# A depthwise convolution whose running sums move to PSUM and whose diagonals move to GpSimd

## The chip, the core and the metric

The kernel runs on one core of one Trainium2 chip. The metric is the device time of one execution in microseconds: the median of three runs of the kernel before is 2928.71 us (2927.53 to 2931.35). The text uses the profile's names of the engines: PE is the matrix engine, PEld its weight load, DVE the vector engine, ACT the scalar engine, POOL is GpSimd, SP issues the loads of the weights.

## The reference

The program is a chain of three blocks over 256 tokens of width 1024, in float32. The change is in the convolution module of the second block:

```
a, gate = split(x @ w_in + b_in)          # 1024 -> 2 x 1024
h = a * sigmoid(gate)
h[t, ch] = b_dw[ch] + sum over w = 0..30 of w_dw[w, ch] * h[t - 30 + w, ch]   # depthwise
h = silu(layer_norm(h)) ;  out = h @ w_out + b_out
```

Everything ahead of it (a feed-forward layer) and behind it stays as it is.

## The kernel before

The module works with channels on partitions: 1024 channels are 8 blocks (`cb`) of 128, and the free dimension is time. `hp` holds for each block 30 zeros and then the 256 gated values, so a tap `w` of the convolution is the slice `hp[:, cb, w:w+256]`, times one weight per partition (`wd`). Four ways of summing the 31 taps are used beside each other:

- blocks 0 to 3, and 23 taps of block 4, on DVE: a chain of instructions, each of which multiplies a tap with its weight and adds the sum so far (`chain`, L1127 and L1131); the sum `y` lies in SBUF;
- block 5 on ACT and POOL: ACT multiplies a tap into a small buffer (three of them, L1163), POOL adds it to `y` (L1166);
- blocks 6 and 7, and 8 taps of block 4, on PE: 70 products with diagonal matrices `dg` that hold the weights, added up in PSUM (`pc`, L1171). DVE builds 30 of these diagonals (L1147), ACT 40 (L1153).

The input product comes in two ways. `stat_pairs` streams eight weight chunks. The first two (the lead) are multiplied for each half of the tokens as soon as its norm is done, and turned by PE transposes (L284); the other six are multiplied as pairs of 2 x 24 matmuls (`mm3`: each product as three, L117 to L119). Each chunk is loaded by SP into `raw` (three buffers), rounded by ACT to `wh` (L99) and the rest computed as `wl` (L101), in two halves: on DVE for chunks 0 to 2, on POOL for chunks 3 to 7. After each pair ACT takes the sigmoid (`sg`, L1150), DVE makes `hp` (L1151), and `advance(12)` traces 12 steps of the chains, in turn over all of them. The pair's PSUM buffer (`acc`, four of them) comes free only behind `hp`.

Behind the sums, 16 transposes (L1180) bring `y` back to tokens on partitions, the layer norm follows (ACT, DVE, and small POOL operations), then the output product, whose first two chunks have their `wl` on POOL.

Tiles are allocated by tag with a fixed number of buffers. A planner orders each engine's queue ahead of the run, by the order in which the code traces the instructions and by its own clock; `issue_after(x)` forbids that instructions traced in its block come ahead of `x` on `x`'s engine. On the chip each queue runs in order. Ahead of the module, `pre_norm` of the second token half ends with two small POOL operations (`rstd`, L147 and L150), on which its transposes wait.

Of the kernel before, what the change touches and what calls it, by code (L numbers as in the profile page):

```python
# [7 lines left out]
F32 = mybir.dt.float32  # L8
# [6 lines left out]
AF = mybir.ActivationFunctionType  # L15
OP = mybir.AluOpType
# [3 lines left out]
S = 256  # L20
D = 1024
# [1020 lines left out]
class Block2:  # L1042
# [61 lines left out]
    def conv(self):  # L1104
        k, nc, a = self.k, self.k.nc, self.k.a
        with ExitStack() as ctx:
            k.temp(ctx, "cvt")
            pool = ctx.enter_context(k.tc.tile_pool(name="cv", bufs=1))
            tl = lambda n, sh, dt=F32: pool.tile(sh, dt, name=n)
            par, wd = tl("par", [128, 3, 8]), tl("wd", [128, 8, 31])  # L1110
            nc.scalar.dma_start(par, a["conv_par"])
            nc.scalar.dma_start(wd, a["conv_dw"])
            lng, lnb, bout = (k.row(n) for n in ("conv_ln_g", "conv_ln_b", "conv_b_out"))
            hp = tl("hp", [128, 8, S + 30])
            nc.gpsimd.memset(hp[:, :, 0:30], 0.0)
            y = tl("y", [128, 8, S])
            xs = [tl(f"xs{t}", [128, D]) for t in range(2)]


            diag = {cb: tl(f"dg{cb}", [128, n, 128]) for cb, n in ((6, 31), (7, 31), (4, 8))}  # L1120
            fill = [(cb, w) for cb in diag for w in range(diag[cb].shape[1])]
            tap = lambda cb, w: hp[:, cb, w:w + S]
            chains = []

            def chain(cb):
                w0 = 8 if cb == 4 else 0
                nc.vector.tensor_scalar(y[:, cb], tap(cb, w0), wd[:, cb, w0:w0 + 1], par[:, 2, cb:cb + 1],  # L1127
                                        op0=OP.mult, op1=OP.add)
                yield
                for w in range(w0 + 1, 31):  # L1130
                    nc.vector.scalar_tensor_tensor(y[:, cb], tap(cb, w), wd[:, cb, w:w + 1], y[:, cb],  # L1131
                                                   op0=OP.mult, op1=OP.add)
                    yield

            def advance(n):

                while n > 0 and chains:
                    c = chains.pop(0)
                    if next(c, 1) is None:
                        chains.append(c)  # L1140
                        n -= 1

            pairs = k.stat_pairs(lambda cb: k.stream(a["conv_in"][cb], pool=cb > 2), 8,
                                 2, lambda c, t: xs[t][:, c * 256:c * 256 + 256])
            with k.tc.issue_after(k.done.ins):
                for b, w in fill[:30]:
                    nc.vector.tensor_scalar(diag[b][:, w], k.ident, wd[:, b, w:w + 1], None, op0=OP.mult)  # L1147
            for cb, (pa, pg) in enumerate(pairs):
                sg = k.tmp.tile([128, S], F32, tag="sg", name="sg")
                ins = nc.scalar.activation(sg, pg, AF.Sigmoid, bias=par[:, 1, cb:cb + 1])  # L1150
                nc.vector.scalar_tensor_tensor(hp[:, cb, 30:], pa, par[:, 0, cb:cb + 1], sg, op0=OP.add, op1=OP.mult)  # L1151
                for b, w in fill[30 + cb * 5:35 + cb * 5]:
                    nc.scalar.activation(diag[b][:, w], k.ident, AF.Copy, scale=wd[:, b, w:w + 1])  # L1153
                if cb < 5:
                    chains.append(chain(cb))
                advance(12)
            scratch = k.sm.tile([128, 1], F32, tag="va", name="scratch")
            nc.scalar.activation(scratch, hp[:, 7, 30:31], AF.Silu)
            with k.tc.issue_after(ins.ins):
                cb = 5  # L1160
                for w in range(31):
                    p = k.tmp.tile([128, S], F32, tag="tap", name="tap", bufs=3) if w else y[:, cb]
                    nc.scalar.activation(p, tap(cb, w), AF.Identity, scale=wd[:, cb, w:w + 1],  # L1163
                                         bias=0.0 if w else par[:, 2, cb:cb + 1])
                    if w:
                        nc.gpsimd.tensor_tensor(y[:, cb], y[:, cb], p, op=OP.add)  # L1166
            for cb in diag:
                n = diag[cb].shape[1]
                pc = k.acc((128, S), "pc")
                for w in range(n):  # L1170
                    nc.tensor.matmul(pc, diag[cb][:, w], tap(cb, w), start=w == 0, stop=w == n - 1)  # L1171
                if cb != 4:
                    nc.scalar.activation(y[:, cb], pc, AF.Identity, bias=par[:, 2, cb:cb + 1])
            advance(155)
            nc.vector.tensor_tensor(y[:, 4], y[:, 4], pc, op=OP.add)
            pts, nms = [], []
            for t in range(2):
                pts.append([k.tp(name="pt") for h in range(2)])
                for cb in range(8):
                    nc.tensor.transpose(pts[t][cb // 4][:, cb % 4], y[:, cb, t * 128:t * 128 + 128], k.ident)  # L1180
                nm = k.sm.tile([128, 1], F32, tag="nm", name="nm")
                sums = k.sm.tile([128, 2], F32, tag="sums", name="sums")
                x = [p.rearrange("p i c -> p (i c)") for p in pts[t]]
                nc.scalar.activation(xs[t][:, 0:512], x[0], AF.Identity, accum_out=sums[:, 0:1])
                nc.vector.tensor_reduce(sums[:, 1:2], x[1], axis=AX.X, op=OP.add)
                nc.vector.tensor_scalar(nm, sums[:, 0:1], sums[:, 1:2], -1.0 / D, op0=OP.add, op1=OP.mult)
                nms.append(nm)
            for t in range(2):
                nm = nms[t]
                ss = k.sm.tile([128, 2], F32, tag="ss", name="ss")  # L1190
                z, sq = k.xn(), k.xn()
                x, u, g, b = ([p.rearrange("p i c -> p (i c)") for p in pts[t]], k.halves(z), k.halves(lng), k.halves(lnb))
                for h, q in enumerate(k.halves(sq)):
                    nc.scalar.activation(q, x[h], AF.Square, bias=nm, accum_out=ss[:, h:h + 1])
                    nc.vector.scalar_tensor_tensor(u[h], x[h], nm, g[h], op0=OP.add, op1=OP.mult)
                sv = k.sm.tile([128, 1], F32, tag="nv", name="nv")
                nc.gpsimd.tensor_tensor(sv, ss[:, 0:1], ss[:, 1:2], op=OP.add)
                r = k.rsqrt_n(sv, D, 1)
                for h, o in enumerate(k.halves(xs[t])):
                    nc.vector.scalar_tensor_tensor(u[h], u[h], r, b[h], op0=OP.mult, op1=OP.add)  # L1200
                    nc.scalar.activation(o, u[h], AF.Silu)
                    k.to_T(o, k.xh, k.xl, t, 4, kb0=h * 4)
                if t == 0:
                    after = k.done
            g3, gn = self.gain(0, 3), self.gain(0, 4)

            def done(t, acc):
                u = [xs[t][:, h * 512:(h + 1) * 512] for h in range(2)]
                for h in range(2):
                    nc.vector.tensor_tensor(u[h], acc[h], bout[:, h * 512:(h + 1) * 512], op=OP.add)  # L1210
                k.post_norm(t, u, g3, 1.0, gn)
            k.last = after
            k.linear_rows(a["conv_out"], k.xh, k.xl, done, tail=2, pool=2)
            k.last = None
# [146 lines left out]
class Block3:  # L1361
# [257 lines left out]
    def mix(self, l, nt):  # L1619
        k, nc, a = self.k, self.k.nc, self.k.a  # L1620
        with ExitStack() as ctx:
# [15 lines left out]
            def attention():  # L1637
                flush()
                for t in (2, 0, 1)[3 - nt:]:
                    yield from self.attention(l, t, sink, ga)  # L1640
            side, conv = attention(), self.conv(l, nt)
            weave(iter(lambda: next(conv, True), True), side, lambda i: 2)
            for _ in side:
                pass
# [225 lines left out]
```

## Time and profile before

| | |
|---|---|
| median of three runs | 2928.71 us |
| the profiled execution's own time | 2930.06 us |
| its span | 2928.3 us |
| PE busy in the span | 2782.8 us (95%) |
| DVE | 1808.6 us (62%) |
| ACT | 1362.3 us (47%) |
| POOL | 437.6 us (15%) |
| granted clock of PE, mean | 0.972 |

Busy time is of one profiled execution. Matmuls overlap, so a busy PE counts each one's whole duration; the distance of two starts is what one costs in a dense row. A number in brackets behind a row is how long the engine sat idle before it and what ended that. "L1131" is a line of the kernel before.

### The profile page before, as it was taken

To read this page: it belongs to the slowest core of one execution; us is meant where nothing else is said; L and a number is where in the kernel's file an instruction comes from. 1 tells how busy PE (TensorE), PEld (TensorE's weight loads), DVE (VectorE), ACT (ScalarE), POOL (GpSimd) and SP (SyncE) were. 2 spreads that over 40 slices of the span, in tenths; PEclk is the share of its full clock that TensorE was granted. 3 is DMA by queue.
4 is the path that set the end of the run, shared out by engine and by line. 5 is a ranking of instruction groups with operands and counts; after the bars stand their busy time and mean duration, and the time that the engine had idled before them with its cause. 6 is when DMAs were issued, how large, how long until landed. Compare 5 with 4: busy or idle time off the path is not lost.

```text
span 2928.3 us, 44693 instructions
## 1 busy us (share of the span) xinstructions
PE 2782.8 (95%) x18182; PEld 2498.8 (85%) x18182; DVE 1808.6 (62%) x2984; ACT 1362.3 (47%) x2318; POOL 437.6 (15%) x338
## 2 busy tenths in 40 slices
PE   8999978899999999998599999999999999999999
PEld 6787978899999888987489899897998878888897
DVE  6646789785555556549765465676655564464654
ACT  4544535544444555435344454524445344453543
POOL 2101766500000000006600000051001010000100
PEclk9999989999999999999799999999999999998999
DMA  5424436696666555554055465524554334442453
GB/s 201 170 72 146 152 129 226 234 336 227 213 206 206 196 188 212 187 187 145 8 197 184 166 214 185 194 89 151 195 187 164 104 107 158 157 143 101 153 189 106
DMA packets 105982, 496.74 MB, mean 170 GB/s; under 512 B 11040, under 2 KB 44320, under 8 KB 50224
## 3 DMA queue, kind: packets, MB, share of 16 engines
q1 hardware_dynamic: 61632, 443.15, 43.7%
q10 hardware_dynamic: 44144, 50.74, 5.2%
q8 instruction: 142, 2.33, 0.3%
q14 instruction: 64, 0.52, 0.0%
HBM read 476.03 MB, written 17.83 MB: 169 GB/s over the span
## 4 chain that ended last, share of the span: by engine, by line
PE 58%; issue 23%; DVE 10%; POOL 4%; DMA 2%; ACT 2%; POOLq 0%; ACTq 0%; DVEq 0%; SPq 0%
PE acc L117 6%; PE acc L119 6%; PE acc L118 6%; PE o L987 4%; PE o L986 4%; PE o L989 4%; PE tp L117 3%; PE tp L119 3%; PE tp L118 3%; PE o L316 2%; DVE y L1131 2%; PE o L319 2%; PE o L317 2%; PE tp L409 2%; DVE A L950 1%
## 5 line engine op out<-in xcount | busy, mean ns | idle before, releaser
L101 DVE TENSOR_TENSOR wl<-raw,wh 128x1024 fp32r<-128x1024 f32 x764 | 914.8, 1218 | 618.3 <-ACT wh L99 617.4
L99 ACT CAST wh<-raw 128x1024 fp32r<-128x1024 f32 x848 | 861.6, 1041 | 709.7 <-PE acc L118 219.1
L117 PE MATMUL acc<-xx,wh 128*128 128x256 f32 x1504 | 423.9, 282 | 3.7 <-DVE hp L1151 3.7
L119 PE MATMUL acc<-xx,wl 128*128 128x256 f32 x1504 | 423.9, 282 | 2.2 <-POOL wl L101 1.4
L118 PE MATMUL acc<-xx,wh 128*128 128x256 f32 x1504 | 424.3, 282 | 0.0
L117 PE MATMUL tp<-xx,wh 128*128 128x256 f32 (+1 forms) x1440 | 413.3, 287 | 5.3 <-ACT ga L970 5.3
L119 PE MATMUL tp<-xx,wl 128*128 128x256 f32 (+1 forms) x1440 | 411.1, 285 | 0.8 <-POOL wl L101 0.8
L118 PE MATMUL tp<-xx,wh 128*128 128x256 f32 (+1 forms) x1440 | 410.9, 285 | 0.0
L147 POOL TENSOR_SCALAR va<-ss 128x1 f32<-128x1 f32 (+1 forms) x49 | 24.6, 502 | 1815.6 <-ACT junk L143 1632.4
L117 PEld LDWEIGHTS acc<-xx,wh 128*128 128x128 f32 x1504 | 285.5, 190 | 3.9 <-issue 3.9
L119 PEld LDWEIGHTS acc<-xx,wl 128*128 128x128 f32 x1504 | 285.6, 190 | 2.6 <-POOL wl L101 1.6
L117 PEld LDWEIGHTS tp<-xx,wh 128*128 128x128 f32 x1440 | 276.6, 192 | 8.8 <-ACT ga L970 5.7
L118 PEld LDWEIGHTS acc<-xx,wh 128*128 128x128 f32 x1504 | 283.8, 189 | 0.0
L118 PEld LDWEIGHTS tp<-xx,wh 128*128 128x128 f32 x1440 | 276.9, 192 | 2.4
L119 PEld LDWEIGHTS tp<-xx,wl 128*128 128x128 f32 x1440 | 276.3, 192 | 1.1 <-POOL wl L101 1.0
L101 POOL TENSOR_TENSOR wl<-raw,wh 128x1024 fp32r<-128x1024 f32 x84 | 236.2, 2836 | 127.1 <-ACT wh L99 127.1
L117 PE MATMUL acc<-wh,xx 128*128 128x256 f32 (+2 forms) x672 | 226.3, 338 | 3.2 <-ACT xx L112 3.2
L118 PE MATMUL acc<-wl,xx 128*128 128x256 f32 (+2 forms) x672 | 221.6, 331 | 4.1 <-DVE wl L101 4.1
L119 PE MATMUL acc<-wh,xx 128*128 128x256 f32 (+2 forms) x672 | 220.4, 331 | 1.2 <-DVE xx L113 1.2
L986 PE MATMUL o<-wh,wth 128*128 128x512 f32 x512 | 200.3, 391 | 0.0
L987 PE MATMUL o<-wl,wth 128*128 128x512 f32 x512 | 199.8, 390 | 0.4 <-DVE wl L101 0.4
L989 PE MATMUL o<-wh,wtl 128*128 128x512 f32 x512 | 159.3, 390 | 0.0
(481 smaller groups left out, 4959.3 us busy)
## 6 DMA issues: line engine op xcount, KB each, us to landing
raw<-in_ffn_in_dram SPq DMA_DIRECT2D x88, 1024.0 KB, 4.9
raw<-in_peer_u_dram SPq DMA_DIRECT2D x64, 1024.0 KB, 5.0
raw<-in_peer_v_dram SPq DMA_DIRECT2D x64, 1024.0 KB, 4.9
raw<-in_ffn_out_dram SPq DMA_DIRECT2D x44, 1024.0 KB, 4.9
raw<-in_w_up_dram SPq DMA_DIRECT2D x32, 1024.0 KB, 4.9
raw<-in_w_down_dram SPq DMA_DIRECT2D x32, 1024.0 KB, 4.9
gd<-gt ACTq DMA_DIRECT2D x16, 1024.0 KB, 4.7
G<-gd ACTq DMA_DIRECT2D x16, 1024.0 KB, 7.2
```

What stands on the lines that cost most here:

```text
L99: nc.scalar.copy(h[:, c], r[:, c])
L101: eng.tensor_tensor(l[:, c], r[:, c], h[:, c].bitcast(F32), op=OP.subtract)
L117: mm(out, ah, bh, start=start, stop=False)
L118: mm(out, ah, bl, start=False, stop=False)
L119: mm(out, al, bh, start=False, stop=stop)
L316: mm(acc[t][h], hi[:, k, ts], wv[0][:, h], start=st, stop=False)
L317: mm(acc[t][h], hi[:, k, ts], wv[1][:, h], start=False, stop=False)
L319: mm(acc[t][h], lo[:, k, ts], wv[0][:, h], start=False, stop=sp)
L409: k.pe = nc.tensor.matmul(ps[:, i, f:f + n], q(h), kt, start=True, stop=mask is None)
L986: mm(acc[t][h], wh, vh[:, h], start=st, stop=False)
L987: mm(acc[t][h], wh, vl[:, h], start=False, stop=False)
L989: mm(acc[t][h], wl, vh[:, h], start=False, stop=sp)
```

## The change

The diagonals are no longer built by DVE and ACT: 14 `affine_select` instructions on POOL write them, seven at a time (each keeps the weight where row and column agree and fills zero elsewhere). They belong to blocks 7, 6 and 23 taps of block 5, 85 in all. The chains of blocks 0 to 3 and of the last 8 taps of block 5 keep their sums in PSUM: two `ya` buffers of tag `tq` hold two blocks each, and an `acc` buffer the third chain; only the last step writes SBUF. `y` is no tile of its own any more, it lies over `hp`. Block 4 goes to ACT and POOL. `advance(8)` takes the place of `advance(12)`, two chains in turn instead of all. All eight chunks of the input product have `wl` on DVE. The products run in the order 5, 6, 7, and the transposes are queued behind the last one of them; ACT's taps are queued behind the last sigmoid, as the taps of block 5 were before.

```diff
--- before.py
+++ after.py
@@ -1111,24 +1111,32 @@
             nc.scalar.dma_start(par, a["conv_par"])
             nc.scalar.dma_start(wd, a["conv_dw"])
             lng, lnb, bout = (k.row(n) for n in ("conv_ln_g", "conv_ln_b", "conv_b_out"))
+            xs = [tl(f"xs{t}", [128, D]) for t in range(2)]
             hp = tl("hp", [128, 8, S + 30])
             nc.gpsimd.memset(hp[:, :, 0:30], 0.0)
-            y = tl("y", [128, 8, S])
-            xs = [tl(f"xs{t}", [128, D]) for t in range(2)]
-
-
-            diag = {cb: tl(f"dg{cb}", [128, n, 128]) for cb, n in ((6, 31), (7, 31), (4, 8))}
-            fill = [(cb, w) for cb in diag for w in range(diag[cb].shape[1])]
+
+
+            first = 23
+            y = hp[:, :, 30:]
+            ysum, y5 = tl("ysum", [128, S]), tl("y5", [128, S])
+            diag = {cb: tl(f"dg{cb}", [128, n, 128]) for cb, n in ((7, 31), (6, 31), (5, first))}
+            for cb in (5, 6, 7):
+                n = diag[cb].shape[1]
+                for w in range(0, n, 7):
+                    d = diag[cb][:, w:min(w + 7, n)]
+                    m = d.shape[1]
+                    nc.gpsimd.affine_select(d, wd[:, cb, w:w + m, None].to_broadcast([128, m, 128]), pattern=[[0, m], [-1, 128]],
+                                            base=0, channel_multiplier=1, compare_op=OP.is_equal, fill=0.0)
             tap = lambda cb, w: hp[:, cb, w:w + S]
             chains = []
 
-            def chain(cb):
-                w0 = 8 if cb == 4 else 0
-                nc.vector.tensor_scalar(y[:, cb], tap(cb, w0), wd[:, cb, w0:w0 + 1], par[:, 2, cb:cb + 1],
+            def chain(cb, w0, acc, out):
+
+                nc.vector.tensor_scalar(acc, tap(cb, w0), wd[:, cb, w0:w0 + 1], par[:, 2, cb:cb + 1],
                                         op0=OP.mult, op1=OP.add)
                 yield
                 for w in range(w0 + 1, 31):
-                    nc.vector.scalar_tensor_tensor(y[:, cb], tap(cb, w), wd[:, cb, w:w + 1], y[:, cb],
+                    nc.vector.scalar_tensor_tensor(out if w == 30 else acc, tap(cb, w), wd[:, cb, w:w + 1], acc,
                                                    op0=OP.mult, op1=OP.add)
                     yield
 
@@ -1137,47 +1145,50 @@
                 while n > 0 and chains:
                     c = chains.pop(0)
                     if next(c, 1) is None:
-                        chains.append(c)
+                        chains.insert(min(1, len(chains)), c)
                         n -= 1
 
-            pairs = k.stat_pairs(lambda cb: k.stream(a["conv_in"][cb], pool=cb > 2), 8,
-                                 2, lambda c, t: xs[t][:, c * 256:c * 256 + 256])
-            with k.tc.issue_after(k.done.ins):
-                for b, w in fill[:30]:
-                    nc.vector.tensor_scalar(diag[b][:, w], k.ident, wd[:, b, w:w + 1], None, op0=OP.mult)
+            def taps():
+
+                for w in range(31):
+                    p = k.tmp.tile([128, S], F32, tag="tap", name="tap", bufs=3) if w else ysum
+                    nc.scalar.activation(p, tap(4, w), AF.Identity, scale=wd[:, 4, w:w + 1],
+                                         bias=0.0 if w else par[:, 2, 4:5])
+                    if w:
+                        nc.gpsimd.tensor_tensor(y[:, 4] if w == 30 else ysum, ysum, p, op=OP.add)
+                    yield
+
+            ya = [k.tp((128, 2, S), name="ya", tag="tq") for i in range(2)]
+            pairs = k.stat_pairs(lambda cb: k.stream(a["conv_in"][cb]), 8, 2, lambda c, t: xs[t][:, c * 256:c * 256 + 256])
             for cb, (pa, pg) in enumerate(pairs):
                 sg = k.tmp.tile([128, S], F32, tag="sg", name="sg")
-                ins = nc.scalar.activation(sg, pg, AF.Sigmoid, bias=par[:, 1, cb:cb + 1])
+                gate = nc.scalar.activation(sg, pg, AF.Sigmoid, bias=par[:, 1, cb:cb + 1])
                 nc.vector.scalar_tensor_tensor(hp[:, cb, 30:], pa, par[:, 0, cb:cb + 1], sg, op0=OP.add, op1=OP.mult)
-                for b, w in fill[30 + cb * 5:35 + cb * 5]:
-                    nc.scalar.activation(diag[b][:, w], k.ident, AF.Copy, scale=wd[:, b, w:w + 1])
-                if cb < 5:
-                    chains.append(chain(cb))
-                advance(12)
+                if cb < 4:
+                    chains.append(chain(cb, 0, ya[cb // 2][:, cb % 2], y[:, cb]))
+                advance(8)
+            with k.tc.issue_after(gate.ins):
+                for _ in taps():
+                    pass
             scratch = k.sm.tile([128, 1], F32, tag="va", name="scratch")
             nc.scalar.activation(scratch, hp[:, 7, 30:31], AF.Silu)
-            with k.tc.issue_after(ins.ins):
-                cb = 5
-                for w in range(31):
-                    p = k.tmp.tile([128, S], F32, tag="tap", name="tap", bufs=3) if w else y[:, cb]
-                    nc.scalar.activation(p, tap(cb, w), AF.Identity, scale=wd[:, cb, w:w + 1],
-                                         bias=0.0 if w else par[:, 2, cb:cb + 1])
-                    if w:
-                        nc.gpsimd.tensor_tensor(y[:, cb], y[:, cb], p, op=OP.add)
-            for cb in diag:
+            chains.append(chain(5, first, k.acc((128, S), "ya5"), y5))
+            for cb in (5, 6, 7):
                 n = diag[cb].shape[1]
                 pc = k.acc((128, S), "pc")
                 for w in range(n):
-                    nc.tensor.matmul(pc, diag[cb][:, w], tap(cb, w), start=w == 0, stop=w == n - 1)
-                if cb != 4:
+                    prod = nc.tensor.matmul(pc, diag[cb][:, w], tap(cb, w), start=w == 0, stop=w == n - 1)
+                if cb == 5:
+                    advance(155)
+                    nc.vector.tensor_tensor(y[:, cb], pc, y5, op=OP.add)
+                else:
                     nc.scalar.activation(y[:, cb], pc, AF.Identity, bias=par[:, 2, cb:cb + 1])
-            advance(155)
-            nc.vector.tensor_tensor(y[:, 4], y[:, 4], pc, op=OP.add)
             pts, nms = [], []
             for t in range(2):
                 pts.append([k.tp(name="pt") for h in range(2)])
-                for cb in range(8):
-                    nc.tensor.transpose(pts[t][cb // 4][:, cb % 4], y[:, cb, t * 128:t * 128 + 128], k.ident)
+                with k.tc.issue_after(prod.ins):
+                    for cb in range(8):
+                        nc.tensor.transpose(pts[t][cb // 4][:, cb % 4], y[:, cb, t * 128:t * 128 + 128], k.ident)
                 nm = k.sm.tile([128, 1], F32, tag="nm", name="nm")
                 sums = k.sm.tile([128, 2], F32, tag="sums", name="sums")
                 x = [p.rearrange("p i c -> p (i c)") for p in pts[t]]
```

## Rows read from the trace of the kernel before

**Rows 1.** Page, part 2: busy tenths of PE in 40 slices of the span.
```profile
PE   8999978899999999998599999999999999999999
```

**Rows 2.** Windows of the stage: length, PE, PEld, DVE, ACT, POOL busy (instructions), clock, DMA.
```profile
1383.00:1411.00 28.00, 8.20 (x31) 6.75 (x30) 28.00 (x58) 7.31 (x13) 10.95 (x7) 0.63 0.22 75
...
1436.00:1454.00 18.00, 1.06 (x8) 0.50 (x6) 1.59 (x3) 12.11 (x24) 16.19 (x23) 0.66 0.00 0
1454.00:1466.00 12.00, 8.10 (x29) 6.63 (x30) 10.33 (x16) 7.37 (x18) 2.51 (x6) 0.51 0.23 79
```

**Rows 3.** Chain of waits, 1310 to 1500 us: start, us, what ran.
```profile
1343.67 2.27 DVE wl L101 x2
...
1398.22 4.75 DVE y L1131 x12
...
1411.54 22.91 issue
...
1453.19 0.73 POOL y L1166
1453.97 1.56 PE pt L1180 x6
```

**Rows 4.** Timeline of DVE and POOL: start, us, engine, line, operation, count, idle before.
```profile
1335.54 8.13 DVE L1147 TENSOR_SCALAR dg<-ident,wd 128x128 f32<-128x128 f32 x30
...
1350.70 19.43 DVE L1131 SCALAR_TENSOR_TENSOR y<-hp,wd,y 128x256 f32<-128x256 f32 x11
...
1344.34 23.93 POOL L101 TENSOR_TENSOR wl<-raw,wh 128x1024 fp32r<-128x1024 f32 x9 [0.95 <-ACT wh L99]
...
1411.24 23.17 POOL L1166 TENSOR_TENSOR y<-y,tap 128x256 f32<-128x256 f32 x1 [4.22 <-ACT tap L1163]
```

**Rows 5.** By tile (`hp`, `pt`, `wl`): ns min/median/max, first and last start, forms.
```profile
L1131 DVE SCALAR_TENSOR_TENSOR y<-hp,wd,y x142: 468/474/2635, 1350.7 to 1436.5; 128x256 f32<-128x256 f32 x142
...
L1151 DVE SCALAR_TENSOR_TENSOR hp<-acc,par,sg x8: 464/470/472, 1345.9 to 1410.0; 128x256 f32<-128x256 f32 x8
...
L1195 DVE SCALAR_TENSOR_TENSOR xn<-pt,nm,row x4: 739/742/743, 1457.3 to 1460.8; 128x512 f32<-128x512 f32 x4
...
L101 POOL TENSOR_TENSOR wl<-raw,wh x14: 2392/2582/6771, 1341.0 to 1384.5; 128x1024 fp32r<-128x1024 f32 x14
```

**Rows 6.** Timeline of PE: lead's end, a pair, the stalls, the products.
```profile
1340.37 0.28 PE L119 MATMUL acc<-wh,xx 128*128 128x256 f32 x1
...
1341.05 0.73 PE L284 MATMUL acc<-ident,xs 128*128 128x128 f32 x4
...
1363.88 0.28 PE L119 MATMUL acc<-xx,wl 128*128 128x256 f32 x1
...
1366.72 0.28 PE L119 MATMUL acc<-xx,wl 128*128 128x256 f32 x1
1370.68 0.55 PE L117 MATMUL acc<-xx,wh 128*128 128x256 f32 x1 [3.68 <-DVE hp L1151]
...
1403.41 16.87 PE L1171 MATMUL pc<-hp,dg 128*128 128x256 f32 x67 [19.80 <-DVE hp L1151]
...
1419.69 16.36 PE L1171 MATMUL pc<-hp,dg 128*128 128x256 f32 x75
```

**Rows 7.** POOL's groups by form, whole span: count, busy us, mean ns, idle before.
```profile
L1166 POOL TENSOR_TENSOR y<-y,tap 128x256 f32<-128x256 f32 x30 | 47.7, 1592 | 19.2 <-ACT tap L1163 17.0
...
masks.py:199 POOL TENSOR_SCALAR_AFFINE_SELECT ident<-ident 128x128 f32<-128x128 f32 x1 | 0.3, 292 | 0.0
...
L1382 POOL TENSOR_SCALAR_AFFINE_SELECT mmeta<-mmeta 128x16 bf16<-128x16 bf16 x1 | 0.2, 200 | 0.1
```

**Rows 8.** Timeline of POOL and ACT: the pre-norm's `va`, the issue of `wd`.
```profile
1331.44 0.36 POOL L147 TENSOR_SCALAR va<-ss 128x1 f32<-128x1 f32 x1 [2.46 <-ACT junk L143]
...
1327.57 0.46 ACTq L1112 DMA_DIRECT2D wd<-in_conv_dw_dram  x1
```

**Rows 9.** DMA issues, 1310 to 1500 us: count, size, median us to landing.
```profile
wd<-in_conv_dw_dram ACTq DMA_DIRECT2D x1, 124.0 KB, 4.6
```

## The prediction

> **What bounds the kernel now.** The page's table of slices comes first: PE is busy in nine tenths or more of nearly every slice, and the one hole that belongs to the changed code are slices 19 and 20 (8 and 5 tenths) [rows 1]. The windows of that stretch, second, show it by phase: from 1383 to 1411 us PE works 8.20 of 28 us while DVE works all of it, and from 1436 to 1454 only 1.06 of 18 us while POOL works 16.19 [rows 2]. Third, the chain of waits names what runs in the holes: first DVE, with its splits and convolution steps, and from 1411.54 POOL, blocked for 22.91 us and then adding 24 taps until 1453.92; the transposes that the layer norm needs start at 1453.97 [rows 3]. Two causes are to be seen.
>
> First, DVE and POOL hold each other up. Alone, 12 convolution steps take 4.75 us, 0.396 us each [rows 3]. Beside POOL's nine `wl` subtractions 11 steps take 19.43 us, and in the opposite direction one POOL add of the tap sum lasts 23.17 us while DVE runs its steps without a gap [rows 4]. But the eight `hp` products (L1151), which read one operand from PSUM and one from SBUF, last 464 to 472 ns each, though the first start at 1345.9 in POOL's busy stretch (1344.34 and 23.93 us); the steps with two SBUF operands reach 2635 ns [rows 4, 5]. So one SBUF operand goes free and two are blocked.
>
> Second, because `hp` comes late from this DVE, PE idles 3.68 us and then 19.80 us, and the tap sum, whose last 24 adds take 0.81 us each, ends last, 18 us after the 70 diagonal products (their last 75 passes end at 1436.05) [rows 3, 6].
>
> **The change, part by part.** The sum starts at 1335.6 us, where the pre-norm of the second half is done, and ends where the transposes start; behind that point the code is the same.
>
> PE. The second half of the lead ends at about 1340.7 [rows 6]; transposes of the lead's rows bring it to 1341.2 and a little more, the last four start at 1341.05. Six pairs remain, 6 x 48 = 288 matmuls at 2.84/24 = 0.1183 us [rows 6], 34.1 us: 1375.3 without a stall. The products become 31 + 31 + 23 = 85 instead of 70, each two passes; 75 passes took 16.36 us [rows 6], 0.216 per pass (74 intervals in 16.36 - 0.38), so 85 x 0.432 = 36.8 us. The end is 1412.1 plus whatever stalls PE (d). The 15 added products cost 6.5 us of that and are paid on the path.
>
> DVE. Taken away: the 30 diagonals (8.13 us) [rows 4] and 15 of 147 steps (5.9 us). Added: 10 `wl` halves that POOL did, 10 x 1.14 us (two take 2.27) [rows 3] = 11.4 us. Until the last `hp` it has 12 halves (13.7), 8 `hp` (3.2) and 7 x 8 = 56 steps (22.2): 39.1 us, so 1374.7, abreast of PE. Then 132 - 56 = 76 steps are left, 30.1 us: DVE ends near 1405, under the products. Per pair DVE needs 2.3 + 0.4 + 3.2 = 5.9 us against PE's 5.7; it has almost no slack.
>
> A step that writes PSUM isn't in the trace. Its lower end is the 0.396 us of the SBUF step, the upper end the 742 ns of a step over twice as many elements, half of them from PSUM [rows 5], as if read and write went one after the other. I take 0.42, since the `hp` products with a PSUM operand last as long as the SBUF steps (470 and 474 ns): 132 x 0.024 = 3 us more, behind cover. At 0.742 DVE would end at 1335.6 + 13.7 + 3.2 + 98 = 1450.5.
>
> The Trainium skill, "Perfetto Trace Analysis", section "Optimizing Scalar/DVE Operations", speaks against sums in PSUM: it gives a DVE access some 60 ns of overhead on SBUF and some 125 ns on PSUM. By that page, an estimate, 132 steps would cost 8.6 us more and DVE would end near 1414, about level with the products. For reads the trace does not show the difference (470 against 474 ns); for writes no run here shows it yet.
>
> POOL. Taken away: 10 of its 14 `wl` halves; the four of `conv_out` stay (2.58 us in the median, 10.3 us) [rows 5]. Added: 14 selects that build 85 blocks of 128 x 128. The trace has one block at 292 ns and one of 16 columns at 200 [rows 7], 0.82 ns a column: 85 x 128 x 0.82 + 14 x 0.19 = 11.6 us. The other end is 292 ns for each block, 24.8 us; I take 14, as it is the same instruction. They wait for `wd`, issued at 1327.57, 4.6 us to landing [rows 8, 9]: 1332.2 to about 1346, at worst 1360. The first product is wanted at 1375, so they are covered. What they can hurt: the pre-norm's `va` of the second half runs on POOL at 1331.44 [rows 8]. If a select stands ahead of it in POOL's queue, it waits for `wd` and for that select: 1332.2 + 1.0 (or 2.1) against 1331.44, 2 to 4 us, and PE, which has nothing else then, waits as long. And four to six `wl` halves (two SBUF operands) each wait up to one select: 3 to 8 us of DVE, partly passed on to PE. I put d = 4 us: 2 for `va`, 2 for DVE's lag; its bounds are 0 and 10.
>
> ACT. Taken away: 40 diagonals. The taps stood behind the last sigmoid already (the code before has the same `issue_after` there), so this part of the title moves nothing by itself; only the block of channels is another (4 for 5), and POOL is freed from DVE's two-operand steps. Last sigmoid near 1379 (d included), then 30 adds at 0.80 us: the sum ends at 1404, or at 1414 if the four `conv_out` halves fall in between. Both are under the products' end, the second by 2 us.
>
> Transposes behind the last product. Before, six of the 16 ran ahead, behind the products, and the next six stand in the chain behind POOL's last add [rows 3]; nothing else was blocked by them. The order gives nothing back, and costs 0.7 us: 16 follow one another where 10 were left.
>
> Sum: the products end at 1412.1 + 4 = 1416. Transposes start there instead of at 1453.97, 0.7 us is lost: 37.3 us gained. The profiled execution took 2930.06 us, 1.35 above the median of 2928.71; 2930.06 - 37.3 = 2892.8, by the median 2891.4. I say **2893**. The slow clock at 1454 to 1466 (granted 0.51) [rows 2] I leave as it is: 3.68 us of idling already slowed a matmul from 0.28 to 0.55 us [rows 6], and the wait of the layer norm stays longer than that.
>
> **The rivals.**
> Half of it (DVE or POOL paces). If a PSUM step costs between 0.5 and 0.67 us, DVE ends at 1335.6 + 16.9 + 66 (88) = 1418 to 1441; or the adds keep their mean of 1.59 us (47.7/30) [rows 7] and end at 1379 + 48 = 1427. Gain 12 to 35 us, time 2896 to 2918. For it: DVE has no slack against PE, and everything is in order in one queue.
> The lock stays. If what blocks is not the second SBUF operand, DVE is blocked by 14 selects (14 us) and POOL by 56 steps: `hp` ends near 1390, DVE near 1425, and POOL can add only then, 24 us, 1449: gain 4 us, 2925. Against it: the `hp` rows.
> Slower. The step in PSUM costs more than 0.77 us. This is the point: 1335.6 + 16.9 + 132 x 0.767 = 1453.7, from there DVE ends later than POOL does now. At 0.85 us it is 1464.7, some 11 us slower, 2940. For it: no row has DVE writing PSUM, and reading and writing meet in one bank. Against: PSUM reads cost nothing extra.
> The order does nothing. True of both orderings in the title, as shown; the gain must come from the PSUM sums and from moving the diagonals and `wl`.
>
> **How the numbers follow.** The forecast 0.58 (2887 to 2903), half of it 0.25 (2903 to 2918), the lock 0.08, slower 0.06, and 0.03 for a larger gain than PE's floor allows (d = 0 and a warm clock behind: 2886). A change under 0.2%, 5.9 us, can't be told from none. Faster: 0.58 + 0.25 + 0.03 and a fifth of the lock, 0.88; within: the rest of the lock and of the edge of "slower", 0.07; slower 0.05. The range that leaves out no more than 2 in 10: 2886 to 2914; the bounds of d (0 to 10) and of the PSUM step up to 0.65 us lie in it.
>
> **What would show it.** Steps on `ya` near 0.4 to 0.45 us while POOL is busy, none above 1 us; selects about 1 us each, done before 1360; `va` of the second half near 1331.5 (else d); PE without a hole from 1341 to the last product near 1416; the last tap add before it; DVE's chain done before it. The prediction is wrong if PE idles in the products' stretch, if the tap sum or the chain ends behind the last product, or if `hp` 5 comes after the last pair.

## The result and the profile after

The changed kernel takes 2897.69 us (median of 4 runs, 2893.43 to 2902.06) against 2929.57 us (4 runs) for the kernel before: ratio 0.9884, 95% interval 0.9872 to 0.9896, 1.2% faster. The profiled execution took 2895.30 us, its span is 2893.5.

Whole times of one kernel spread by up to 16 us, and in the eleven profiles the changed code starts anywhere from 1323.16 to 1329.14 us. So the experiments below are also compared by the **stage**, read from one profiled execution each: from the start of the `hp` memset on POOL to the layer norm's first square on ACT. Before it is 1327.13 to 1456.14 = 129.0 us, after 1328.90 to 1422.75 = 93.9 us, and 93.9 again in a second run of the changed kernel. The gain of 35.1 us is the stage's; the memset starts 1.8 us later and 1.4 us are gained behind the stage, which makes the 34.8 us between the two spans. Times of after are 1.8 us late against before for that reason.

In the page's table of slices the hole of slices 19 and 20 (8 and 5 tenths) [rows 1] is gone:

```profile
PE   8999978899999999999999999999999999999999
```

The windows of the stage (length, PE, PEld, DVE, ACT, POOL busy with instructions, clock, DMA) answer to [rows 2]:

```profile
1334.00:1341.00 7.00, 2.22 (x13) 1.61 (x12) 2.31 (x2) 0.49 (x2) 6.82 (x9) 0.80 0.26 105
1341.00:1346.00 5.00, 5.00 (x28) 4.74 (x27) 4.26 (x4) 3.04 (x5) 5.00 (x6) 0.60 0.01 3
...
1352.00:1385.00 33.00, 33.00 (x278) 32.87 (x277) 32.41 (x69) 14.89 (x20) 9.54 (x4) 1.00 0.63 221
1385.00:1421.00 36.00, 36.00 (x171) 31.53 (x170) 31.91 (x80) 18.73 (x37) 21.83 (x30) 1.00 0.00 0
```

From 1352 to 1421 PE works all of 69 us at the full clock, where before it had 8.20 of 28 and 1.06 of 18. One hole is left, at 1334 to 1341, with a slow clock (0.60) behind it. PE's timeline names its cause, and shows products and transposes without a gap, against [rows 6] and the transposes of [rows 3]:

```profile
1339.55 2.23 PE L205 MATMUL tp<-ident,xn 128*128 128x128 f32 x8 [4.78 <-DVE xn L165]
...
1383.84 36.87 PE L1180 MATMUL pc<-hp,dg 128*128 128x256 f32 x170
1420.55 1.99 PE L1191 MATMUL pt<-ident,hp 128*128 128x128 f32 x16
1426.89 1.97 PE L205 MATMUL tp<-ident,xs 128*128 128x128 f32 x8 [4.35 <-ACT xs L1212]
```

By tile, against [rows 5], the steps that sum in PSUM (`ya`) never exceed 490 ns; the blocked 2635 is gone:

```profile
L1139 DVE SCALAR_TENSOR_TENSOR ya<-hp,wd,ya x122: 476/483/490, 1354.2 to 1416.5; 128x256 f32<-128x256 f32 x122
...
L1166 DVE SCALAR_TENSOR_TENSOR hp<-acc,par,sg x8: 476/480/485, 1353.1 to 1385.4; 128x256 f32<-128x256 f32 x8
L1135 DVE TENSOR_SCALAR ya<-hp,wd,par x5: 541/543/547, 1353.6 to 1407.7; 128x256 f32<-128x256 f32 x5
```

DVE and POOL now work side by side, against [rows 4]. First DVE's timeline, then POOL's:

```profile
1338.31 2.31 DVE L165 TENSOR_SCALAR xn<-xn,ya 128x512 f32<-128x512 f32 x2 [4.89 <-POOL ya L150]
...
1385.78 14.19 DVE L1139 SCALAR_TENSOR_TENSOR ya<-hp,wd,ya 128x256 f32<-128x256 f32 x36
...
1416.98 0.48 DVE L1139 SCALAR_TENSOR_TENSOR hp<-hp,wd,ya 128x256 f32<-128x256 f32 x1
```

```profile
1334.01 2.85 POOL L1128 TENSOR_SCALAR_AFFINE_SELECT dg<-wd 128x896 f32<-128x896 f32 x3 [3.24 <-DMA wd<-in_conv_dw_dram]
1336.96 0.30 POOL L147 TENSOR_SCALAR va<-ss 128x1 f32<-128x1 f32 x1
1337.33 0.41 POOL L1128 TENSOR_SCALAR_AFFINE_SELECT dg<-wd 128x256 f32<-128x256 f32 x1
1337.70 0.57 POOL L150 TENSOR_TENSOR ya<-va,half 128x1 f32<-128x1 f32 x1
...
1386.31 23.29 POOL L1158 TENSOR_TENSOR ysum<-ysum,tap 128x256 f32<-128x256 f32 x29 [7.84 <-ACT tap L1155]
```

36 steps take 14.19 us, 0.394 each, while POOL adds without a pause at 23.29/29 = 0.80 us; before, one add lasted 23.17 us beside steps whose sum lay in SBUF. The second timeline also shows what is still lost: three selects, which wait for `wd`, stand ahead of the second half's `va` in POOL's queue, and a fourth, short one stands between `va` and its root.

### The profile page after: what moved, and what is told of

Same layout as the page of the kernel before. It is cut to its first block, busy times and chain, and to the rows that moved or that the text cites. A ratio compares the mean times of both kernels' runs of the same rounds, so it can differ in the third digit from the quotient of the medians.

```text
span 2893.5 us, 44686 instructions
## 1 busy us (share of the span) xinstructions
PE 2786.3 (96%) x18212; PEld 2502.2 (86%) x18212; DVE 1779.9 (62%) x2949; ACT 1351.9 (47%) x2278; POOL 401.2 (14%) x342
## 5 line engine op out<-in xcount | busy, mean ns | idle before, releaser
L101 DVE TENSOR_TENSOR wl<-raw,wh 128x1024 fp32r<-128x1024 f32 (+1 forms) x774 | 928.7, 1221 | 620.1 <-ACT wh L99 619.2
L101 POOL TENSOR_TENSOR wl<-raw,wh 128x1024 fp32r<-128x1024 f32 x74 | 205.3, 2796 | 130.2 <-ACT wh L99 130.1
```

The source lines that it names most:

```text
L101: eng.tensor_tensor(l[:, c], r[:, c], h[:, c].bitcast(F32), op=OP.subtract)
```

## The experiments

**The lock, from both sides.** First the PSUM sums alone, in the kernel before: diagonals, `wl` and orders stay (block 4's sum is started behind the pairs, as it has to have a PSUM tile of its own).

```diff
...
-nc.vector.scalar_tensor_tensor(y[:, cb], tap(cb, w), wd[:, cb, w:w + 1], y[:, cb],
+nc.vector.scalar_tensor_tensor(y[:, cb] if w == 30 else acc, tap(cb, w), wd[:, cb, w:w + 1], acc,
...
-                if cb < 5:
-                    chains.append(chain(cb))
+                if cb < 4:
+                    chains.append(chain(cb, ya[cb // 2][:, cb % 2]))
...
+            chains.append(chain(4, k.acc((128, S), "ya4")))
```

> The kernel before, with one part of the change alone: the chains of blocks 0 to 3 and the 23 taps of block 4 sum up in PSUM (the last one is started behind the pairs). Diagonals on DVE and ACT, wl of chunks 3 to 7 on POOL, advance(12) and all orders as before. Theory (the whole gain is that DVE's steps no longer fight with POOL): DVE 1335.6 + 8.1 + 2.3 + 3.2 + 84 x 0.394 = 1382 for the last hp, 70 products of 30.2 us end near 1414, the tap sum near 1408, so transposes near 1415 instead of 1454: 30 to 39 us faster than before, 2891 to 2900. Rival (the gain needs the diagonals and wl off DVE, ACT and POOL as well): at most half, 2911 or more.

Measured: 2891.16 us, ratio 0.9866 (0.9844 to 0.9887); stage 1328.07 to 1418.84 = 90.8 us, 38.2 less than before, inside the 30 to 39 expected. In its timeline (POOL and DVE, picked rows) POOL's thirteen `wl` halves take 2.48 us each in the mean (the shortest one before took 2.39 [rows 5]), while the convolution steps beside them take 0.40 us:

```profile
1345.31 32.25 POOL L101 TENSOR_TENSOR wl<-raw,wh 128x1024 fp32r<-128x1024 f32 x13 [0.96 <-ACT wh L99]
...
1363.24 5.18 DVE L1131 SCALAR_TENSOR_TENSOR ya<-hp,wd,ya 128x256 f32<-128x256 f32 x13
...
1387.40 9.88 DVE L1131 SCALAR_TENSOR_TENSOR ya<-hp,wd,ya 128x256 f32<-128x256 f32 x25
...
1405.62 9.93 DVE L1131 SCALAR_TENSOR_TENSOR ya<-hp,wd,ya 128x256 f32<-128x256 f32 x19
```

The last of these rows, 0.52 us a step, is block 4's sum alone; it is taken up at the end. The place of the sums alone makes the whole gain, and 3 us more than the change does. Second, the changed kernel with its sums back in SBUF:

```diff
-            ya = [k.tp((128, 2, S), name="ya", tag="tq") for i in range(2)]
+            ya = [xs[i][:, 512:].rearrange("p (e s) -> p e s", e=2) for i in range(2)]
...
-            chains.append(chain(5, first, k.acc((128, S), "ya5"), y5))
+            chains.append(chain(5, first, y5, y5))
```

> The changed kernel with its running sums in SBUF again (in unused halves of xs, and y5); all else as it is, though the planner, which counts other times for SBUF, orders DVE's queue a little differently. Theory (lock between POOL and steps with two SBUF operands): steps beside the selects and POOL's wl take 1 to 2.6 us, hp comes late, and the tap adds are blocked until DVE's chain is done, so they end near 1450: 25 to 38 us slower than the changed kernel, 2922 to 2935. Rival (the gain came from the moved diagonals and wl): within 5 us of the changed kernel.

Measured: 2916.29 us, ratio 0.9948 (0.9927 to 0.9969); stage 112.3 us, 18.4 more than the changed kernel. Its timeline (DVE, POOL, PE):

```profile
1374.00 5.95 DVE L1139 SCALAR_TENSOR_TENSOR xs<-hp,wd,xs 128x256 f32<-128x256 f32 x4
...
1383.02 2.57 DVE L1139 SCALAR_TENSOR_TENSOR xs<-hp,wd,xs 128x256 f32<-128x256 f32 x1
...
1394.80 0.48 DVE L1166 SCALAR_TENSOR_TENSOR hp<-acc,par,sg 128x256 f32<-128x256 f32 x1 [1.00 <-ACT sg L1165]
...
1395.92 30.89 DVE L1139 SCALAR_TENSOR_TENSOR xs<-hp,wd,xs 128x256 f32<-128x256 f32 x42
...
1373.86 5.02 POOL L101 TENSOR_TENSOR wl<-raw,wh 128x1024 fp32r<-128x1024 f32 x2 [28.00 <-ACT wh L99]
...
1395.73 25.18 POOL L1158 TENSOR_TENSOR ysum<-ysum,tap 128x256 f32<-128x256 f32 x29 [10.43 <-ACT tap L1155]
...
1367.90 0.39 PE L119 MATMUL acc<-xx,wl 128*128 128x256 f32 x1 [2.74 <-DVE wl L101]
...
1371.95 1.53 PE L1180 MATMUL pc<-hp,dg 128*128 128x256 f32 x6 [1.19 <-DVE hp L1166]
...
1386.78 0.58 PE L119 MATMUL acc<-xx,wl 128*128 128x256 f32 x1 [7.89 <-DVE wl L101]
```

The lock is back. Beside POOL's last `wl` halves three DVE steps (two of the four in the first row) take 2.6 us each and the tensor_scalar that opens a sum 2.43, PE waits 7.89 us for the `wl` behind them, and the last `hp` comes 71.1 us behind the memset instead of 56.5. The 42 steps after it take 0.74 us each in the mean, and the windows (as in [rows 2]) show them at two paces, beside POOL's adds and behind them:

```profile
1396.00:1421.00 25.00, 25.00 (x117) 21.90 (x116) 25.00 (x30) 15.44 (x30) 22.73 (x30) 1.00 0.00 1
1422.00:1426.70 4.70, 4.70 (x24) 4.11 (x23) 4.70 (x13) 2.43 (x4) 0.00 (x0) 1.00 0.00 0
```

Here the engines take turns, one step to one add, 0.87 us each, and POOL is nearly as fast as alone (0.80). So the direction held and the size, 25 to 38 us, was too large: I had carried over POOL's starvation from [rows 4]. Why POOL starves there and takes its turn here was not tried. Not all of the 18.4 us is the lock either: PE's waits of 2.74 and 1.19 us for DVE fall into the 28.00 us in which POOL is idle. The planner had put DVE's queue in another order.

The four stages together: 129.0 before, 90.8 with PSUM alone, 112.3 with all but PSUM, 93.9 with both. The parts don't add: alone the rest of the change gains 16.7 us, but beside the PSUM sums it costs 3 us, as it stands.

**The transposes' order.** The changed kernel without it:

```diff
-                with k.tc.issue_after(prod.ins):
-                    for cb in range(8):
-                        nc.tensor.transpose(pts[t][cb // 4][:, cb % 4], y[:, cb, t * 128:t * 128 + 128], k.ident)
+                for cb in range(8):
+                    nc.tensor.transpose(pts[t][cb // 4][:, cb % 4], y[:, cb, t * 128:t * 128 + 128], k.ident)
```

> The changed kernel without the order that queues the transposes behind the last product. My prediction said that this order gives nothing back. Against it stands the queue that the planner writes without it: 23 products of block 5, then three transposes, of blocks 0 to 2, then the other 62 products. PE comes to them at about 1394 us, and DVE writes blocks 0 to 2 at 1400.4, 1407.4 and 1411.8. So this theory expects PE to idle some 18 us there, plus 1 to 3 us of slow clock behind it: 17 to 21 us slower than the changed kernel, about 2916 us. If the prediction's step was right: within 2 us of the changed kernel.

Measured: 2917.33 us (8 runs), ratio 0.995 (0.9935 to 0.9964); stage 113.6 us, 19.7 more. PE's timeline:

```profile
1378.20 10.10 PE L1180 MATMUL pc<-hp,dg 128*128 128x256 f32 x46
1404.82 0.90 PE L1190 MATMUL pt<-ident,hp 128*128 128x128 f32 x3 [16.52 <-POOL hp L1158]
1405.52 29.50 PE L1180 MATMUL pc<-hp,dg 128*128 128x256 f32 x124
```

Without the order three transposes are queued between block 5's 23 products (46 passes) and the other 62 (124 passes). PE waits 16.52 us at them, with 27 us of products behind it. The wait ends with POOL's last add of block 4, and not with DVE's sums, as I had expected. Behind it the granted clock is 0.50 up to 1410, and the 124 passes take 29.50 us where 124 x 0.216 = 26.8. Expected 17 to 21 us: held.

**The taps' order.** The changed kernel without it:

```diff
-            with k.tc.issue_after(gate.ins):
-                for _ in taps():
-                    pass
+            for _ in taps():
+                pass
```

> The changed kernel without the order that holds ACT's taps behind the last sigmoid. The planner then puts 8, 13 and 9 taps between the sigmoids of blocks 4 to 7, and two of POOL's wl halves behind the adds. The taps are paced by POOL's adds (0.80 us), so the last sigmoids come 5 to 12 us later. Theory (as predicted, the order gives nothing by itself): the products of block 5 fill PE for 9.9 us behind the last pair and those of block 6 for 13.4 us, which covers the late hp 6 and 7; within 3 us of the changed kernel. Rival (late sigmoids hold back hp, and with it the PSUM buffers and PE): 5 to 12 us slower.

Measured: 2904.03 us, ratio 0.9896 (0.9875 to 0.9918); stage 104.2 us, 10.3 more: the theory (within 3 us) missed. Its timelines (ACT, then DVE, then PE):

```profile
1376.95 0.51 ACT L1155 ACTIVATE tap<-hp,wd 128x256 f32<-128x256 f32 x1 [0.31 <-POOL ysum L1158]
1377.37 0.46 ACT L1165 ACTIVATE sg<-acc,par 128x256 f32<-128x256 f32 x1
...
1387.94 0.46 ACT L1165 ACTIVATE sg<-acc,par 128x256 f32<-128x256 f32 x1
...
1397.08 0.47 ACT L1165 ACTIVATE sg<-acc,par 128x256 f32<-128x256 f32 x1
```

```profile
1388.43 0.48 DVE L1166 SCALAR_TENSOR_TENSOR hp<-acc,par,sg 128x256 f32<-128x256 f32 x1 [5.72 <-ACT sg L1165]
1397.58 0.48 DVE L1166 SCALAR_TENSOR_TENSOR hp<-acc,par,sg 128x256 f32<-128x256 f32 x1 [4.36 <-ACT sg L1165]
```

```profile
1384.02 36.87 PE L1179 MATMUL pc<-hp,dg 128*128 128x256 f32 x170
1420.73 0.38 PE L1190 MATMUL pt<-ident,hp 128*128 128x128 f32 x2
...
1430.50 3.04 PE L1190 MATMUL pt<-ident,hp 128*128 128x128 f32 x13 [5.22 <-DVE hp L1139]
```

The taps, which go at the pace of POOL's adds, stand ahead of the last three sigmoids; the last `hp` comes at 1397.58 instead of 1385.38, and DVE, idle for 13.6 us in three waits, ends its sums behind the products. The rival's number (5 to 12 us) came out, but not its way: PE's products start at 1384.02 and run without a gap, as in the changed kernel (1383.84); it is the transposes that wait for DVE.

**What the selects and `wl` cost.** Three kernels from the changed one: `wl` of the later blocks on POOL again; the 85 diagonals built as before, 30 on DVE and 55 on ACT, without selects; and the selects queued behind the second half's `va` and its root, by an order on that instruction.

```diff
-            pairs = k.stat_pairs(lambda cb: k.stream(a["conv_in"][cb]), 8, 2, ...
+            pairs = k.stat_pairs(lambda cb: k.stream(a["conv_in"][cb], pool=cb > 2), 8, 2, ...
```

> The changed kernel with wl of chunks 3 to 7 on POOL, as before. POOL does the ten halves behind the selects, from about 1351 us, at 2.4 to 2.6 us each: 4.8 to 5.2 us a chunk against PE's 5.7 us a pair, just in time; DVE is freed of 11 us. Theory (the lock concerns two SBUF operands only, so moving wl was no part of the gain): within 2 us of the changed kernel, DVE's chain done some 10 us ahead of the last product. Rival (wl had to leave POOL): PE waits for wl in several pairs, 5 us slower or more.

```diff
...
-                    nc.gpsimd.affine_select(d, wd[:, cb, w:w + m, None].to_broadcast([128, m, 128]), ...
...
+            with k.tc.issue_after(k.done.ins):
+                for b, w in fill[:30]:
+                    nc.vector.tensor_scalar(diag[b][:, w], k.ident, wd[:, b, w:w + 1], None, op0=OP.mult)
...
+                for b, w in fill[30 + cb * 7:37 + cb * 7]:
+                    nc.scalar.activation(diag[b][:, w], k.ident, AF.Copy, scale=wd[:, b, w:w + 1])
```

> The changed kernel with its 85 diagonals built as before, 30 on DVE ahead of the pairs and 55 on ACT between them, no selects on POOL. Theory: nothing stands ahead of va any more (some 7 us less), but 8.1 us of DVE come back in front of wl of chunk 2 (PE waits about 3 us) and before the last hp, so DVE's chain ends near the last product: 2 to 5 us faster than the changed kernel. So the selects bring nothing where they stand. Rival (the diagonals had to leave DVE and ACT): 4 us slower or more.

```diff
-        nc.gpsimd.tensor_tensor(y, v, self.half[:p, 0:1], op=OP.pow)
+        self.pw = nc.gpsimd.tensor_tensor(y, v, self.half[:p, 0:1], op=OP.pow)
...
-                    nc.gpsimd.affine_select(d, wd[:, cb, w:w + m, None].to_broadcast([128, m, 128]), ...
+                    with k.tc.issue_after(k.pw.ins):
+                        nc.gpsimd.affine_select(d, wd[:, cb, w:w + m, None].to_broadcast([128, m, 128]), ...
...
```

> The changed kernel, with the 14 selects held behind the last pow of the pre-norm on POOL. Theory (the selects ahead of `va` delay the second half of the pre-norm: PE idles 4.78 us before its transposes and then runs some 24 passes at the slow clock): the 4.78 us go, and with them about 2 us of slow clock, so 5 to 7 us faster than the changed kernel, some 2891 us against 2897. The rest of the stage shifts ahead as a whole, since PE has no hole behind that point. Rival (DVE paces, as it has under 1 us of idle time up to the last hp, and the selects now block its wl halves): under 2 us faster.

Measured: `wl` on POOL 2897.32 us, stage 93.7: no difference, as expected; DVE ends 8.7 us ahead of the products. Diagonals on DVE and ACT 2894.55 us, stage 89.5, 4.4 less (expected 2 to 5); PE waits 0.95 us for a `wl` where I expected 3. Late selects 2889.27 us, ratio 0.9863 (0.9837 to 0.9888), stage 88.4, 5.5 less (expected 5 to 7). Late selects' timeline of POOL, of DVE and of PE:

```profile
1327.48 0.36 POOL L147 TENSOR_SCALAR va<-ss 128x1 f32<-128x1 f32 x1 [2.46 <-ACT junk L143]
1327.92 0.56 POOL L150 TENSOR_TENSOR ya<-va,half 128x1 f32<-128x1 f32 x1
1328.44 18.85 POOL L1129 TENSOR_SCALAR_AFFINE_SELECT dg<-wd 128x896 f32<-128x896 f32 x14
```

```profile
1328.52 2.30 DVE L165 TENSOR_SCALAR xn<-xn,ya 128x512 f32<-128x512 f32 x2 [0.85 <-POOL ya L150]
```

```profile
1329.76 0.66 PE L205 MATMUL tp<-ident,xn 128*128 128x128 f32 x4 [0.75 <-DVE xn L165]
1330.87 0.66 PE L205 MATMUL tp<-ident,xn 128*128 128x128 f32 x4 [0.46 <-DVE xn L165]
```

PE waits 0.75 and 0.46 us for the pre-norm instead of 4.78, and its clock stays at 1.00 in the windows from 1328 to 1346. The selects still cost something where `va` is not held up: DVE's two pre-norm operations beside them take 2.30 us, as in the changed kernel, against 0.88 alone.

**The best of it.** Late selects with three taps of block 5 moved from the products to DVE's sum, beside a second run of the changed kernel on the same chip. The edit, against late selects:

```diff
-            first = 23
+            first = 20
```

> Selects behind the second `va`, and three taps of block 5 taken from PE's products for DVE's sum (first = 20 for 23): 82 diagonals for 85. In the run with the selects behind `va` the products ended at 1409.5, DVE's chain at 1406.6 and POOL's adds at 1399.3. If PE's products alone set the end, 3 x 0.432 = 1.3 us are gained in the stretch, 87.1 for 88.4 us, with DVE's chain ending at 1406.6 + 3 x 0.394 = 1407.8, still ahead of the products' 1408.2. The rival: with 0.4 us between the two, DVE's last step of block 5 comes late for the transposes, and nothing or less than 0.5 us is gained. The whole time, 2888 us, cannot tell the two apart, the stretch can.

> The changed kernel again, as the yardstick on the same chip as the two runs beside it. By the stretch from the memset of `hp` to the layer norm's first square it should need 93.9 us as before, give or take 0.5; by the whole time 2895 to 2900 us. The theory that the selects ahead of the second `va` cost 5 to 6 us needs it 5 to 6 us longer in that stretch than a kernel that queues the selects behind `va`; the rival, that the two earlier whole times (2897.7 and 2889.3) differ by chance of the rest of the program, needs the same stretch and other lengths elsewhere.

Measured: late selects with `first = 20` 2890.47 us (2888.57 to 2893.06), ratio 0.9861 (0.9845 to 0.9878), stage 87.1; the changed kernel again 2896.38 us (2892.95 to 2899.18), stage 93.9. PE still ends last (1411.9, against DVE's 1411.4), and the 1.3 us are there in the stage; the rival falls. In whole time this version leads the changed kernel by 6 us, and the two sets of four runs overlap by 0.1 us only; from late selects (2889.27) the whole time cannot tell it, only the stage can. The changed kernel needs its 93.9 us again, so the earlier difference between it and late selects was not chance.

## Why the prediction was right, and where not

The forecast, 2893 with its own range 2887 to 2903, held: 2897.69. Its mechanism is shown from both sides (PSUM sums put into the kernel before, and taken out of the changed one). What it credits beside it, the moved diagonals and `wl`, had no part in the gain as it stands. By its steps:

- **PE's floor.** Right: 36.87 us for 170 passes, 36.8 predicted. With d = 0 the transposes would start 1412.1 - 1327.13 = 85.0 us behind the memset; they start 1420.55 - 1328.90 = 91.65 behind it. So **d is 6.7 us where I took 4**: the one term that was mis-sized, inside its bounds. Late selects brings it to 1409.36 - 1323.16 - 85.0 = 1.2. The 5.5 us between are `va`: PE's hole grows from 0.75 and 0.46 to 4.78 us, and 28 matmuls take 5 us at the clock of 0.60 behind it. I had priced `va`'s delay at 2 us, the low end, for one select ahead of it where three came, and left the clock and the pre-norm's own blocking (below) out. The 2 us for DVE's lag did not come: six `wl` halves beside the selects took 10.14 us instead of 6.8, but behind 1341 PE never waited for them.
- **Transposes: 0.7 us lost.** Not so: sixteen take 1.99 us at the full clock where six took 1.56 at a low one [rows 3], and the first square starts 2.20 us behind the first of them, 2.17 before. 37.3 - 2.7 + 0.7 = 35.3, against the stage's 35.1.
- **The PSUM step.** 0.394 us while POOL adds; 0.42 taken. The Trainium skill, "Perfetto Trace Analysis", section "Optimizing Scalar/DVE Operations", gives a DVE access some 125 ns of overhead on PSUM against some 60 on SBUF. Steps that alternate between two sums do not show that difference: 0.394 in PSUM, 0.396 in SBUF [rows 3]. Only the last five on one sum alone took 0.52 (2.58 us from 1414.37), under cover. The tensor_scalar that opens a sum takes longer, 543 ns into PSUM against 397 to 415 unblocked in the run with SBUF sums; what makes the difference no run separates.
- **DVE ends at 1405.** Wrong by 10 us: 1417.5, or 1415.7 less the shift. The 30.1 us behind the last `hp` were nearly right (31.7, 1385.8 to 1417.5); but the last `hp` comes at 1385.4, not at 1374.7: it has to wait for the last pair, which comes late by d, and for its sigmoid. DVE stayed 3 us ahead of the products.
- **"One SBUF operand goes free and two are blocked."** Too simple. The pre-norm's tensor_scalar (one SBUF tensor in, SBUF out) took 2.31 us for two beside the selects, against 0.88 alone. Rows of the kernel before, which I passed over, said so: two of the same kind beside POOL's `wl`, and one of the 30 diagonals, at 2444 ns for 282, beside POOL's first `wl` half. The `hp` products, which also read one SBUF tensor and write SBUF, stay free (485 ns at most); what tells the two forms apart no run separates.

```profile
1346.66 4.12 DVE L1127 TENSOR_SCALAR y<-hp,wd,par 128x256 f32<-128x256 f32 x2
...
L1147 DVE TENSOR_SCALAR dg<-ident,wd x30: 273/282/2444, 1335.5 to 1343.4; 128x128 f32<-128x128 f32 x30
```

- **Selects.** 0.95 us for 896 columns alone, 1.28 in the mean of eleven, some beside DVE (up to 1.96), 16.1 us in all (14 taken), done by 1351: covered.
- **"The order gives nothing back"; the rival "the order does nothing".** This is the step that failed. It was argued from the queue of the kernel before, where the transposes stood behind the products anyway. The changed kernel's queue is another one: without the order three transposes go ahead of 62 products, and it is 19.7 us slower in the stage. The taps' order was no news against before, as I said, but it too carries 10.3 us here. What either order is worth in the kernel before no run shows; in the changed one they keep the transposes and the taps from taking back 20 and 10 of the 35 us. The forecast did not suffer from this step, since the change has both orders and their worth was not in the sum.
- **The other rivals.** No step is near 0.77 us, and only the five on one sum alone are near 0.5; the lock between the sums and POOL went.
- **The sum.** The profiled execution: 2892.8 by the working, + 2.7 (d) - 0.7 (transposes) + 1.8 (the stage starts later) - 1.4 (behind the stage) = 2895.2, measured 2895.30. Of the 1.4 us, 0.87 lie where the first of two sets of transposes leads the second by 4.49 us instead of 5.36, a stretch whose slow clock I had left as it was; the rest was not traced. The start of the stage varies from run to run by more than the whole miss, and the four terms partly cancel, so that the total came within 2.5 us of this execution is in part luck; the mark of the working is the stage, 35.1 us for 37.3. The median lies 2.4 us above that execution, within the spread of the runs.

## What to carry to other kernels

When a two-engine lock bounds a stage, look first for the one operand that can leave SBUF: here that alone gave all of the gain. The work moved between engines beside it cost 3 us of the stage as it stood, and with the selects behind `va` it gave 2.4 (88.4 us for 90.8). Judge an order by the queue that the new code would get without it, not by the queue of the old code. Before work is put on an engine's queue, look for a short link of the critical path that will be queued behind it: three selects ahead of one `va`, with a fourth behind it, cost 5.5 us.

## What the runs showed of the hardware that was not expected

- A tensor_scalar on DVE from SBUF to SBUF is held up by POOL too (2.31 us for 0.88 beside the selects, 2.44 for 0.28 beside a `wl` half), though its second operand is one value per partition; with its output in PSUM it is not (554 ns at most in all runs).
- Steps on one PSUM sum in a row are slower than steps that alternate between two: 19 on the last sum took 9.93 us, 0.52 each, against 9.88/25 = 0.395, in the run with PSUM sums alone. Whether a sum in SBUF does the same no run shows.
- In the lock POOL can be shut out (one add of 23.17 us in the kernel before [rows 4], while DVE's steps run on at 0.396 us), or the two can take turns (30 steps and 30 adds at 0.87 us each in the run with the sums back in SBUF). What decides it stays open.
